# Weight sums in place, a fifth buffer of split weights, and interleaved halves of pairs in a decoder layer of float32 products

## The chip, the cores and the metric

The kernel runs on one core of a Trainium2 chip. The metric is the device time of one launch in microseconds (us), the median of several runs. The engines that matter here are TensorE (PE in the profile, its weight loads PEld), which does the matrix products; ScalarE (ACT) and VectorE (DVE), which prepare its operands; GpSimd (POOL), which issues accumulating transfers on a DMA queue of its own; and SyncE (SP), which issues the loads of all weights.

## The reference

One layer of a decoder, batch 1, 256 positions, model width 2048, in float32:

```
x = x + 0.5 * swiglu(rmsnorm(x, g1), wg1, wu1, wd1)     # swiglu(h) = (silu(h @ wg) * (h @ wu)) @ wd
h = rmsnorm(x, gm);  parts = split(h @ w_in)            # attention and mLSTM inputs
x = x + concat(diff_attention(parts), mlstm(parts)) @ w_out
x = x + 0.5 * swiglu(rmsnorm(x, g2), wg2, wu2, wd2)
return rmsnorm(x, g_final)
```

The hidden width of the two gated feed-forward blocks (FFN 1 and FFN 2) is 5632: 44 rows of 128, or 11 chunks of 512 columns. Each of their six weight matrices has 46 MB and is read once. The change is in the FFNs alone.

## The kernel before

**Products of split numbers.** Every float32 operand is split into a high part (a cast on ScalarE, L113) and a low part (the difference, on VectorE, L114), and each product is three TensorE instructions: high times high (L141), high times low (L142), low times high (L143). The weights are the moving operand, 512 columns wide (128x512, 256 KB of float32 for 128 rows). So each weight has to be loaded, cast and subtracted before TensorE can use it, and the split weights live in the pool wsp, whose buffers (four before) hold two 128x512 tiles, high and low, of "one split".

**Pairs: seven products in place of eight.** The 256 positions are two halves of 128. The class Paired takes two columns of weights wa and wb (gate and up for one chunk of the hidden width, or two chunks of the down matrix) and computes both for both halves. A pair is two rows k, k+1 of both columns, a 2x2 block: B11 = wa row k, B21 = wa row k+1, B12 = wb row k, B22 = wb row k+1. The activations are combined beforehand (A1, A2, B2 and S1 to S4). The weights of a pair are combined here:

- f, one split of two sums: T1 = B11+B12 for the accumulator p5 and T3 = B22+B12 for p7. Before, both are written by one VectorE instruction (L350) to a tile "sums" of the pool wrp (five buffers, which the single units below use too);
- e, one split of B11 for p1 and T2 = T1+B22 for p6 (T2 by VectorE, L352, in B12's place);
- bare, one split of B21 and T4 = T2+B21. T4 is made by an accumulating DMA on GpSimd's queue, 256 KB from one part of the raw tile to another (L361), which adds B21 to T2 in place, once e has read T2;
- upper, one split of the B22 of two pairs.

first() does f and e of each pair of a run, then combine() (L368 to L373) forms sums of the four accumulators: u1 is a copy of p1 (L368, L371 are ScalarE's copies), u2 = p6 + u1 (L369), p7 += u2 (L370), u3 is a copy of p7 (L371), and two subtractions into p6 and p5 (L372, L373). Then second() adds bare, upper and the single units of column wa (p1 and p7), after which these two accumulators are complete; the single units of column wb are left as a stream, third(), that goes on p5 and p6.

**Order.** Chain.run pulls a run's first() one step at a time and between the steps takes from the stream that the run before has left, so that each step of first() is followed by its share of single units. A generator's `yield` is where the stream's units come in. In each FFN there are 18 or 19 runs: 10 or 11 of gate and up (four pairs and four streamed units), and 8 of down, two (c = 0 and c = 2) for each of the four parts into which the hidden width is cut, with three pairs in parts 0 to 2 (and three units of each column) and one pair in part 3 (six chunk rows left as units). That makes 37 runs and 122 pairs.

The order of instructions on each engine is set by a scheduler from the order of the code and from priorities: loads, sums and splits stand under tc.high_priority(AHEAD), 400 places ahead of their place in the code, the combine under soon(), 440 places ahead. On the chip each engine then works through its list in order, and each instruction waits for its semaphores. SyncE's loads wait for a free tile of their pool: wr (four raw tiles of 1 MB, one for each pair) or wrp (tiles of 512 KB: single units, and the sums).

Of the kernel before, what the change touches and what calls it, by code (L numbers as in the profile page):

```python
# [17 lines left out]
P = 128  # L18
# [6 lines left out]
CW = 512  # L25
# [24 lines left out]
def tile_trunk_layer(ctx: ExitStack, tc: tile.TileContext, x, xt, par, bias_if, lamv, fnorm,  # L50
# [6 lines left out]
    wr = ctx.enter_context(tc.tile_pool(name="wr", bufs=4))  # L57
    wrp = ctx.enter_context(tc.tile_pool(name="wrp", bufs=5))
    wsp = ctx.enter_context(tc.tile_pool(name="wsp", bufs=4))
    small = ctx.enter_context(tc.tile_pool(name="small", bufs=2))  # L60
# [103 lines left out]

    def load_pair(dst, w, k):
        nc.sync.dma_start(dst, w[k // LK][:, k % LK:k % LK + 2, :])  # L166

    def load_unit(w, k):
        raw = wrp.tile([P, UK, CW], F32, tag="rawp", name=nm("rawp"))
        with tc.high_priority(offset=AHEAD):  # L170
            load_pair(raw, w, k)
        return raw
# [149 lines left out]
    class Paired:  # L322
# [4 lines left out]

        def __init__(self, xp, wa, wb, nk, ns, w0=0):
            self.xp, self.wa, self.wb, self.k0 = xp, wa, wb, w0 * LK
            self.ns, self.rest = ns, range(2 * ns, nk, UK)  # L330
            self.raws = []

        def prod(self, acc, j, xi, w, wi, first, last, on=False):
            xh, xl = self.xp[j]
            mm3(acc, xh[:, xi, :], xl[:, xi, :], w[0][:, wi, :], w[1][:, wi, :], first, last, on)

        def first(self):


            self.p1, self.p6, self.p7, self.p5 = (bank() for _ in range(4))  # L340
            for j in range(self.ns):
                raw = wr.tile([P, 4, CW], F32, tag="raw", name=nm("raw"))
                self.raws.append(raw)
                at, end = j == 0, j == self.ns - 1
                with tc.high_priority(offset=AHEAD):
                    for i, w in enumerate((self.wa, self.wb)):
                        load_pair(raw[:, 2 * i:2 * i + 2, :], w, self.k0 + 2 * j)
                    f = pair_tiles(wsp, "w", [P, 2, CW])
                    sums = wrp.tile([P, 2, CW], F32, tag="rawp", name=nm("sums"))
                    nc.vector.tensor_tensor(out=sums, in0=raw[:, 0:4:3, :],  # L350
                                            in1=raw[:, 2:3, :].to_broadcast([P, 2, CW]), op=ALU.add)
                    nc.vector.tensor_tensor(out=raw[:, 2, :], in0=sums[:, 0, :], in1=raw[:, 3, :], op=ALU.add)  # L352
                    e = pair_tiles(wsp, "w", [P, 2, CW])
                    split(sums, *f)
                    split(raw[:, 0:3:2, :], *e)
                self.prod(self.p5, j, S1, f, 0, at, end)
                self.prod(self.p7, j, S3, f, 1, at, end)
                self.prod(self.p1, j, A1, e, 0, at, end)
                self.prod(self.p6, j, S2, e, 1, at, end)
                with tc.high_priority(offset=AHEAD):  # L360
                    nc.gpsimd.dma_start(raw[:, 2, :], raw[:, 1, :], accum_op=ALU.add)  # L361
                yield
# [23 lines left out]
        def second(self):  # L386
# [3 lines left out]
            def bare(j):  # L390
                with tc.high_priority(offset=AHEAD):
                    t = pair_tiles(wsp, "w", [P, 2, CW])
                    split(self.raws[j][:, 1:3, :], *t)
                self.prod(n11, j, A2, t, 0, False, False, True)
                self.prod(n21, j, B2, t, 1, False, False, True)

            def upper(j0):
                with tc.high_priority(offset=AHEAD):
                    t = pair_tiles(wsp, "w", [P, 2, CW])
                    js = range(j0, min(j0 + 2, self.ns))  # L400
                    for i, j in enumerate(js):
                        split(self.raws[j][:, 3, :], t[0][:, i, :], t[1][:, i, :])
                for i, j in enumerate(js):
# [58 lines left out]
    def ffn(chain, xp, rstd, wg, wu, wd, finish, first=None):  # L462
# [21 lines left out]
        for part, (n, ns) in enumerate(zip(PARTS, NP_DOWN)):  # L484
# [19 lines left out]
            for c in (0, 2):  # L504
                p = Paired(hid, wd[c], wd[c + 1], n * 4, ns, done)
                if last:
# [517 lines left out]
```

## Time and profile before

The median of three runs is 1823.52 us (1822.75 to 1824.73). The page describes one profiled execution.

| | before |
|---|---|
| profiled execution, device time | 1824.08 us |
| its span in the trace | 1822.4 us |
| granted clock of TensorE, mean | 0.998 |
| TensorE busy | 1794.6 us (98%) in 8090 instructions |
| VectorE busy | 1488.8 us (82%) |
| ScalarE busy | 1121.7 us (62%) |
| GpSimd busy | 156.3 us (9%) |
| queue of the loads, share of 16 DMA engines | 55.5% |
| GpSimd's queue, share of 16 DMA engines | 14.2% |
| read from HBM | 349.56 MB |

How to read it: a row of the waits names the waiting engine, the tile and line that waits, then what it waited for, the time in us, the number of waits and the longest one. A row of the order of time has the start (us from the span's start), the duration, the engine, the line, the operation, what it writes and reads with shapes, and in brackets how long the engine stood before it and for what. A row of the table by stretches has the stretch, its length, the busy time and number of instructions of PE, PEld, DVE, ACT and POOL, TensorE's granted clock, the busy share of the DMA engines, and GB/s.

### The profile page before, as it was taken

What the parts mean: (1) busy time and instruction counts of PE and PEld (TensorE: products, weight loads), DVE (VectorE), ACT (ScalarE), POOL (GpSimd) and SP (SyncE); (2) the same over time, 40 slices, a digit from 0 to 9 for tenths busy, and PEclk for the clock granted to TensorE, in tenths of its full rate; (3) what the DMA queues carried; (4) which work ended last, traced back from release to release, by engine and by line L of the source; (5) the groups of instructions that cost most, each with busy time, mean ns of one, the idle gap of its engine ahead of it and who ended that gap; (6) DMA issues with size and microseconds to landing.
All of it is one profiled execution on the core that took longest, in us unless ns stands there. A gap on an engine that the chain in (4) does not pass through costs nothing.

```text
span 1822.4 us, 22684 instructions
## 1 busy us (share of the span) xinstructions
PE 1794.6 (98%) x8090; PEld 1468.2 (81%) x8090; DVE 1488.8 (82%) x1775; ACT 1121.7 (62%) x1443; POOL 156.3 (9%) x199
## 2 busy tenths in 40 slices
PE   8999999999999999999999999999999999999998
PEld 6788788878887888978888888788787888887886
DVE  6889889988998887674465578899889988998886
ACT  6666666666666666554455456666666666666664
POOL 0001100111002100000000000101110021002100
PEclk9999999999999999999999999999999999999999
DMA  8667877797688874553544565677877798678864
GB/s 333 215 204 235 222 234 232 246 250 220 210 252 247 259 237 146 200 185 121 185 159 164 185 213 179 199 228 241 234 230 225 256 247 243 208 230 256 253 190 155
DMA packets 114449, 397.72 MB, mean 218 GB/s; under 512 B 12960, under 2 KB 12960, under 8 KB 107424
## 3 DMA queue, kind: packets, MB, share of 16 engines
q1 hardware_dynamic: 88560, 349.28, 55.5%
q0 software_dynamic: 24480, 44.58, 14.2%
q10 hardware_dynamic: 1296, 2.42, 0.4%
q8 instruction: 63, 1.03, 0.2%
q14 instruction: 50, 0.41, 0.1%
HBM read 349.56 MB, written 2.10 MB: 193 GB/s over the span
## 4 chain that ended last, share of the span: by engine, by line
PE 76%; DMA 9%; DVE 8%; issue 4%; ACT 2%; SPq 1%; POOL 0%; POOLq 0%; DVEq 0%; ACTq 0%
PE acc L142 24%; PE acc L143 24%; PE acc L141 24%; DMA raw<-in_wu_dram 6%; DVE wl L114 5%; ACT wh L113 2%; DVE sums L350 2%; DMA raw<-raw 1%; PE tr L296 1%; SPq L166 1%; DMA xres<-in_x_dram 1%; DVE raw L352 1%; DMA xraw<-in_xt_dram 1%; DMA raw<-in_wd_dram 0%; PE num L808 0%
## 5 line engine op out<-in xcount | busy, mean ns | idle before, releaser
L113 ACT CAST wh<-raw 128x1024 fp32r<-128x1024 f32 (+3 forms) x503 | 464.3, 931 | 377.2 <-PE acc L143 360.9
L114 DVE TENSOR_TENSOR wl<-raw,wh 128x1024 fp32r<-128x1024 f32 (+3 forms) x503 | 535.1, 1074 | 194.7 <-ACT wh L113 191.1
L142 PE MATMUL acc<-wl,xt 128*128 128x512 f32 (+3 forms) x1632 | 630.4, 386 | 4.2 <-DVE wl L114 4.0
L141 PE MATMUL acc<-wh,xt 128*128 128x512 f32 (+3 forms) x1632 | 630.7, 387 | 2.6 <-ACT xt L108 1.5
L143 PE MATMUL acc<-wh,xt 128*128 128x512 f32 (+3 forms) x1632 | 628.8, 386 | 1.2 <-DVE xt L109 1.2
L114 DVE TENSOR_TENSOR wl<-rawp,wh 128x1024 fp32r<-128x1024 f32 x284 | 346.7, 1222 | 43.8 <-ACT wh L113 37.1
L113 ACT CAST wh<-rawp 128x1024 fp32r<-128x1024 f32 x284 | 298.8, 1053 | 117.1 <-PE acc L143 96.4
L141 PE MATMUL acc<-wh,xs 128*128 128x512 f32 x902 | 355.7, 397 | 8.4 <-ACT wh L113 4.0
L142 PEld LDWEIGHTS acc<-wl,xt 128*128 128x128 f32 x1632 | 306.5, 188 | 67.9 <-DVE wl L114 8.8
L141 PEld LDWEIGHTS acc<-wh,xt 128*128 128x128 f32 x1632 | 306.0, 188 | 65.5 <-ACT wh L113 2.8
L143 PEld LDWEIGHTS acc<-wh,xt 128*128 128x128 f32 x1632 | 306.3, 188 | 62.1 <-DVE xt L109 2.5
L142 PE MATMUL acc<-wl,xs 128*128 128x512 f32 x902 | 352.7, 391 | 1.3 <-DVE wl L114 1.1
L143 PE MATMUL acc<-wh,xs 128*128 128x512 f32 x902 | 350.9, 390 | 0.1
L113 ACT CAST wh<-sums 128x1024 fp32r<-128x1024 f32 x122 | 128.4, 1053 | 144.4 <-PE acc L143 139.2
L141 PEld LDWEIGHTS acc<-wh,xs 128*128 128x128 f32 x902 | 169.1, 188 | 57.2 <-ACT u L371 9.3
L142 PEld LDWEIGHTS acc<-wl,xs 128*128 128x128 f32 x902 | 169.4, 188 | 38.9 <-DVE wl L114 6.4
L143 PEld LDWEIGHTS acc<-wh,xs 128*128 128x128 f32 x902 | 169.3, 188 | 36.0 <-DVE xs L109 1.0
L361 POOL DMA_DIRECT2D raw<-raw x122 | 104.0, 853 | 1030.9 <-DVE wl L114 973.7
L350 DVE TENSOR_TENSOR sums<-raw 128x1024 f32<-128x1024 f32 x122 | 149.2, 1223 | 39.4 <-DMA raw<-in_wu_dram 29.2
L114 DVE TENSOR_TENSOR wl<-sums,wh 128x1024 fp32r<-128x1024 f32 x122 | 149.0, 1222 | 14.7 <-ACT wh L113 14.7
L352 DVE TENSOR_TENSOR raw<-sums,raw 128x512 f32<-128x512 f32 x122 | 83.8, 687 | 0.5
L282 POOL DMA_DIRECT2D xres<-part x48 | 43.6, 1060 | 238.2 <-ACT part L281 238.2
(194 smaller groups left out, 756.0 us busy)
## 6 DMA issues: line engine op xcount, KB each, us to landing
rawp<-in_wd_dram SPq DMA_DIRECT2D x96, 512.0 KB, 5.7
rawp<-in_wu_dram SPq DMA_DIRECT2D x94, 512.0 KB, 7.6
raw<-in_wg_dram SPq DMA_DIRECT2D x89, 512.0 KB, 6.7
rawp<-in_wg_dram SPq DMA_DIRECT2D x86, 512.0 KB, 5.7
raw<-in_wu_dram SPq DMA_DIRECT2D x82, 512.0 KB, 7.5
raw<-in_wd_dram SPq DMA_DIRECT2D x80, 512.0 KB, 6.3
raw<-in_win_dram SPq DMA_DIRECT2D x40, 1024.0 KB, 4.8
raw<-raw POOLq DMA_DIRECT2D x122, 256.0 KB, 6.3
```

The costliest lines, as they stand in the source:

```text
L113: nc.scalar.copy(hi, src)
L114: nc.vector.tensor_tensor(out=lo, in0=src, in1=hi.bitcast(F32), op=ALU.subtract)
L141: nc.tensor.matmul(acc, lh, rh, start=first, stop=False, skip_group_check=on)
L142: nc.tensor.matmul(acc, lh, rl, start=False, stop=False, skip_group_check=on)
L143: nc.tensor.matmul(acc, ll, rh, start=False, stop=last, skip_group_check=on)
L166: nc.sync.dma_start(dst, w[k // LK][:, k % LK:k % LK + 2, :])
L282: nc.gpsimd.dma_start(xres[:, hb, c * CW:(c + 1) * CW], t, accum_op=ALU.add)
L296: nc.tensor.transpose(tr[:, i, hb * P:(hb + 1) * P], hs[hb][:, k * P:(k + 1) * P], ident)
L350: nc.vector.tensor_tensor(out=sums, in0=raw[:, 0:4:3, :], in1=raw[:, 2:3, :].to_broadcast([P, 2, CW]), op=ALU.add)
L352: nc.vector.tensor_tensor(out=raw[:, 2, :], in0=sums[:, 0, :], in1=raw[:, 3, :], op=ALU.add)
L361: nc.gpsimd.dma_start(raw[:, 2, :], raw[:, 1, :], accum_op=ALU.add)
```

## The change

Sums in place. The raw tile of a pair has four places of 256 KB. B11 is loaded to place 3, B12 and B22 to places 1 and 2 by one load of 512 KB. One VectorE instruction writes T3 and T1 to places 0 and 1 (L351 of the changed kernel): the tile "sums" is gone. Once f has split them, T2 = T1 + B22 is made in place 1 (L357; a branch that would let a DMA do it is in the code, but its argument by_dma is False in every run). B21 is loaded late, as a load of its own of 256 KB, to place 0, after f's split has read T3 from there; then GpSimd's accumulating DMA adds it to T2 in place 1 (L371), once e's split has read T2.

Buffers. wsp has five buffers instead of four; wrp has three instead of five.

Order. e of pair j-1 comes after f of pair j, and the places of the `yield`, at which streamed units come in, move. Of three pairs the order is now f0, units, f1, e0, f2, e1, units, e2, units; of four f0, units, f1, e0, units, f2, e1, f3, e2, units, e3, units; of one f0, units, e0. Before it was f0, e0, units, f1, e1, units and so on. bare and upper read other places of the raw tile. The lines of the combine are L387 to L392 now (u2 L388, p7 L389, u3 L390).

```
-    wrp = ctx.enter_context(tc.tile_pool(name="wrp", bufs=5))
-    wsp = ctx.enter_context(tc.tile_pool(name="wsp", bufs=4))
+    wrp = ctx.enter_context(tc.tile_pool(name="wrp", bufs=3))
+    wsp = ctx.enter_context(tc.tile_pool(name="wsp", bufs=5))
...
-    def load_pair(dst, w, k):
-        nc.sync.dma_start(dst, w[k // LK][:, k % LK:k % LK + 2, :])
+    def load_rows(dst, w, k, n):
+        nc.sync.dma_start(dst, w[k // LK][:, k % LK:k % LK + n, :])
...
         def first(self):
             self.p1, self.p6, self.p7, self.p5 = (bank() for _ in range(4))
-            for j in range(self.ns):
+            def f(j):
                 raw = wr.tile([P, 4, CW], F32, tag="raw", name=nm("raw"))
                 self.raws.append(raw)
                 at, end = j == 0, j == self.ns - 1
                 with tc.high_priority(offset=AHEAD):
-                    for i, w in enumerate((self.wa, self.wb)):
-                        load_pair(raw[:, 2 * i:2 * i + 2, :], w, self.k0 + 2 * j)
-                    f = pair_tiles(wsp, "w", [P, 2, CW])
-                    sums = wrp.tile([P, 2, CW], F32, tag="rawp", name=nm("sums"))
-                    nc.vector.tensor_tensor(out=sums, in0=raw[:, 0:4:3, :],
-                                            in1=raw[:, 2:3, :].to_broadcast([P, 2, CW]), op=ALU.add)
-                    nc.vector.tensor_tensor(out=raw[:, 2, :], in0=sums[:, 0, :], in1=raw[:, 3, :], op=ALU.add)
-                    e = pair_tiles(wsp, "w", [P, 2, CW])
-                    split(sums, *f)
-                    split(raw[:, 0:3:2, :], *e)
-                self.prod(self.p5, j, S1, f, 0, at, end)
-                self.prod(self.p7, j, S3, f, 1, at, end)
-                self.prod(self.p1, j, A1, e, 0, at, end)
-                self.prod(self.p6, j, S2, e, 1, at, end)
+                    load_rows(raw[:, 3:4, :], self.wa, self.k0 + 2 * j, 1)
+                    load_rows(raw[:, 1:3, :], self.wb, self.k0 + 2 * j, 2)
+                    t = pair_tiles(wsp, "w", [P, 2, CW])
+                    nc.vector.tensor_tensor(out=raw[:, 0:2, :], in0=raw[:, 2:4, :],
+                                            in1=raw[:, 1:2, :].to_broadcast([P, 2, CW]), op=ALU.add)
+                    split(raw[:, 0:2, :], *t)
+                    if self.by_dma and j < self.ns - 1:
+                        nc.gpsimd.dma_start(raw[:, 1, :], raw[:, 2, :], accum_op=ALU.add)
+                    else:
+                        nc.vector.tensor_tensor(out=raw[:, 1, :], in0=raw[:, 1, :], in1=raw[:, 2, :], op=ALU.add)
+                self.prod(self.p5, j, S1, t, 1, at, end)
+                self.prod(self.p7, j, S3, t, 0, at, end)
+
+            def e(j):
+                raw = self.raws[j]
+                at, end = j == 0, j == self.ns - 1
                 with tc.high_priority(offset=AHEAD):
-                    nc.gpsimd.dma_start(raw[:, 2, :], raw[:, 1, :], accum_op=ALU.add)
+                    t = pair_tiles(wsp, "w", [P, 2, CW])
+                    split(raw[:, 1:4:2, :], *t)
+                self.prod(self.p1, j, A1, t, 1, at, end)
+                self.prod(self.p6, j, S2, t, 0, at, end)
+                with tc.high_priority(offset=AHEAD):
+                    load_rows(raw[:, 0:1, :], self.wa, self.k0 + 2 * j + 1, 1)
+                    nc.gpsimd.dma_start(raw[:, 1, :], raw[:, 0, :], accum_op=ALU.add)
+
+            for j in range(self.ns):
+                f(j)
+                if j:
+                    e(j - 1)
+                if j != self.ns - 2:
+                    yield
+            e(self.ns - 1)
+            if self.ns > 1:
                 yield
...
-                    split(self.raws[j][:, 1:3, :], *t)
+                    split(self.raws[j][:, 0:2, :], *t)
...
-                        split(self.raws[j][:, 3, :], t[0][:, i, :], t[1][:, i, :])
+                        split(self.raws[j][:, 2, :], t[0][:, i, :], t[1][:, i, :])
```

How the order moves. VectorE in FFN 1, the second down run (c = 2) of part 0, three pairs. Before, from e of pair 1 (its raw tile is raw_302) to p7 of the combine; raw_293 and raw_311 are the raw tiles of pairs 0 and 2, rawp a single unit, L350 and L352 the sums of the next run:

```order
L114 TENSOR_TENSOR wl_307_1538<-raw_302_1529,wh_306_1537 128x1024
L114 TENSOR_TENSOR wl_310_1559<-rawp_308_1556,wh_309_1558 128x1024
L114 TENSOR_TENSOR wl_313_1578<-sums_314_1579,wh_312_1577 128x1024
L350 TENSOR_TENSOR sums_353_1752<-raw_350_1747 128x1024
L114 TENSOR_TENSOR wl_316_1583<-raw_311_1574,wh_315_1582 128x1024
L114 TENSOR_TENSOR wl_319_1604<-rawp_317_1601,wh_318_1603 128x1024
L352 TENSOR_TENSOR raw_350_1747<-sums_353_1752,raw_350_1747 128x512
L114 TENSOR_TENSOR wl_326_1635<-raw_293_1484,wh_325_1634 128x1024
L114 TENSOR_TENSOR wl_329_1647<-rawp_327_1644,wh_328_1646 128x1024
L369 TENSOR_TENSOR u2_321_1620<-acc_290_1481,u1_320_1619 128x512
L114 TENSOR_TENSOR wl_331_1663<-raw_302_1529,wh_330_1662 128x1024
L370 TENSOR_TENSOR acc_291_1482<-acc_291_1482,u2_321_1620 128x512
```

After, the same stretch; the raw tiles of pairs 0, 1 and 2 are raw_284, raw_290 and raw_295:

```order
L114 TENSOR_TENSOR wl_299_1560<-raw_290_1517,wh_298_1559 128x1024
L114 TENSOR_TENSOR wl_302_1574<-rawp_300_1571,wh_301_1573 128x1024
L114 TENSOR_TENSOR wl_304_1590<-raw_295_1544,wh_303_1589 128x1024
L114 TENSOR_TENSOR wl_307_1604<-rawp_305_1601,wh_306_1603 128x1024
L114 TENSOR_TENSOR wl_314_1635<-raw_284_1484,wh_313_1634 128x1024
L114 TENSOR_TENSOR wl_317_1647<-rawp_315_1644,wh_316_1646 128x1024
L114 TENSOR_TENSOR wl_319_1663<-raw_290_1517,wh_318_1662 128x1024
L388 TENSOR_TENSOR u2_309_1620<-acc_281_1481,u1_308_1619 128x512
L114 TENSOR_TENSOR wl_321_1673<-raw_284_1484,wh_320_1672 128x512
L389 TENSOR_TENSOR acc_282_1482<-acc_282_1482,u2_309_1620 128x512
```

The first row of each list is the low part of e of pair 1. The second split from the same raw tile is bare of pair 1 (wl_331 before, wl_319 after). Nine rows stand between the two before, five after: f of pair 2 and the next run's sums are no longer among them. u2, the first VectorE step of the combine, stands one row ahead of that bare before, and one row behind it after.

VectorE in FFN 1, the first down run of part 3 (one pair). Before, from e (raw_1178 is the raw tile of the only pair) to bare:

```order
L114 TENSOR_TENSOR wl_1183_5649<-raw_1178_5640,wh_1182_5648 128x1024
L114 TENSOR_TENSOR wl_1186_5670<-rawp_1184_5667,wh_1185_5669 128x1024
L114 TENSOR_TENSOR wl_1189_5688<-rawp_1187_5685,wh_1188_5687 128x1024
L114 TENSOR_TENSOR wl_1192_5706<-rawp_1190_5703,wh_1191_5705 128x1024
L369 TENSOR_TENSOR u2_1197_5740<-acc_1175_5637,u1_1196_5739 128x512
L114 TENSOR_TENSOR wl_1195_5724<-rawp_1193_5721,wh_1194_5723 128x1024
L370 TENSOR_TENSOR acc_1176_5638<-acc_1176_5638,u2_1197_5740 128x512
L350 TENSOR_TENSOR sums_1225_5852<-raw_1222_5847 128x1024
L372 TENSOR_TENSOR acc_1175_5637<-acc_1177_5639,u3_1198_5741 128x512
L373 TENSOR_TENSOR acc_1177_5639<-acc_1177_5639,u2_1197_5740 128x512
L114 TENSOR_TENSOR wl_1200_5751<-raw_1178_5640,wh_1199_5750 128x1024
```

After; raw_1122 is the pair's raw tile, L313 the gated products of the run before:

```order
L114 TENSOR_TENSOR wl_1136_5712<-rawp_1134_5709,wh_1135_5711 128x1024
L114 TENSOR_TENSOR wl_1138_5728<-raw_1122_5640,wh_1137_5727 128x1024
L114 TENSOR_TENSOR wl_1143_5751<-raw_1122_5640,wh_1142_5750 128x1024
L114 TENSOR_TENSOR wl_1145_5761<-raw_1122_5640,wh_1144_5760 128x512
L114 TENSOR_TENSOR wl_1148_5770<-rawp_1146_5767,wh_1147_5769 128x1024
L313 SCALAR_TENSOR_TENSOR sg_1116_5632<-acc_1049_5279,rstd_53_356,sg_1116_5632 128x512
L313 SCALAR_TENSOR_TENSOR sg_1117_5634<-acc_1047_5277,rstd_53_356,sg_1117_5634 128x512
```

Before, four splits of units and the steps of the combine stand between e and bare of the only pair. Now bare follows e directly, and u2 comes after the gated products.

7 lines of the change are left out of this document (4 added, 3 removed).

## The prediction

> **What bounds the kernel now.** I read the page first, then the waits of TensorE, then the order of time around the places where a pair's halves end.
>
> ```profile
> span 1822.4 us, 22684 instructions
> PE 1794.6 (98%) x8090; PEld 1468.2 (81%) x8090; DVE 1488.8 (82%) x1775; ACT 1121.7 (62%) x1443; POOL 156.3 (9%) x199
> PEld acc L142 <- DVE wl L114: 15.1, 25, 1.2
> PEld acc L141 <- ACT wh L113: 10.9, 15, 1.6
> PEld acc L141 <- ACT u L371: 9.3, 25, 1.3
> ACT wh L113 <- PE acc L143: 596.5, 594, 4.3
> 361.00:379.00 18.00, 18.00 (x80) 14.69 (x79) 16.24 (x18) 11.93 (x16) 3.34 (x4) 1.00 0.72 183
> 497.50:532.00 34.50, 34.50 (x158) 28.53 (x157) 33.55 (x39) 22.61 (x27) 2.55 (x3) 1.00 0.84 262
> 569.00:603.60 34.60, 34.02 (x149) 27.26 (x148) 29.74 (x32) 22.40 (x27) 6.86 (x8) 1.00 0.92 259
> ```
>
> TensorE is the bound: it is busy 98% of the span at the full granted clock, and in a stretch without a gap 80 matmuls take 18.0 us, one each 0.226 us. The change leaves their number as it is, so it can only move the gaps. Weights that come late (rows two and three of the waits) hold TensorE's weight loads for 15.1 + 10.9 = 26.0 us in the whole span: no gain can be larger. ScalarE stands 596.5 us in casts that wait for a buffer of split weights to come free, so the four buffers, not ScalarE, set how far the splits run ahead. The last two rows are stages: in 497.5 to 532 us VectorE works 33.55 of 34.50 us, and in 569 to 603.6 us the DMA engines are 92% busy. So three resources stand just behind TensorE.
>
> **What stays the same.** VectorE's work is the same in kind and number.
>
> ```profile
> L350 DVE TENSOR_TENSOR sums<-raw 128x1024 f32<-128x1024 f32 x122 | 149.2, 1223 | 39.4 <-DMA raw<-in_wu_dram 29.2 <-DMA raw<-in_wd_dram 5.5 <-DVE wl L114 2.7
> L352 DVE TENSOR_TENSOR raw<-sums,raw 128x512 f32<-128x512 f32 x122 | 83.8, 687 | 0.5
> L369 DVE TENSOR_TENSOR u<-acc,u 128x512 f32<-128x512 f32 x37 | 25.3, 684 | 0.0
> L371 ACT COPY u<-acc 128x512 f32<-128x512 f32 x37 | 21.4, 579 | 0.6 <-DVE acc L370 0.4
> L313 DVE SCALAR_TENSOR_TENSOR sg<-acc,rstd,sg 128x512 f32<-128x512 f32 x44 | 31.9, 744 | 0.0
> ```
>
> The two sums cost 1.22 us a pair at L350, and T2 0.69 us at L352. The changed kernel does both with as many elements, in place, and the trace has no in-place row to say otherwise; I take the same 1.22 and 0.69. The bytes loaded are the same too. What changes is when things may start.
>
> **Term A: six runs of three pairs with three streamed units** (the second down run of parts 0 to 2, in both FFNs). T4 of each pair is made by an accumulating DMA, which can start once the split e has read T2. So far e follows f directly. Now e of pair 1 comes after f of pair 2, while the combine (u2, p7, u3), on which the second half's products on p7 wait, has moved behind the split of T4 of pair 1 on VectorE, and u1 behind its cast on ScalarE. The run around 360 us, before:
>
> ```profile
> 358.13 1.22 DVE L114 TENSOR_TENSOR wl<-sums,wh 128x1024 fp32r<-128x1024 f32 x1
> 359.26 1.22 DVE L114 TENSOR_TENSOR wl<-raw,wh 128x1024 fp32r<-128x1024 f32 x1
> 361.53 0.69 DVE L352 TENSOR_TENSOR raw<-sums,raw 128x512 f32<-128x512 f32 x1
> 362.13 1.22 DVE L114 TENSOR_TENSOR wl<-sums,wh 128x1024 fp32r<-128x1024 f32 x1
> 363.27 1.22 DVE L114 TENSOR_TENSOR wl<-raw,wh 128x1024 fp32r<-128x1024 f32 x1
> 375.00 0.68 DVE L369 TENSOR_TENSOR u<-acc,u 128x512 f32<-128x512 f32 x1
> 360.56 0.39 PE L142 MATMUL acc<-wl,xs 128*128 128x512 f32 x1
> 378.53 0.50 PE L141 MATMUL acc<-wh,xs 128*128 128x512 f32 x1
> 360.78 1.02 POOL L361 DMA_DIRECT2D raw<-raw  x1
> 364.79 0.84 POOL L361 DMA_DIRECT2D raw<-raw  x1 [1.56 <-DVE wl L114]
> DMA to landing us min/median/max: 7.8/7.8/7.8
> DMA to landing us min/median/max: 9.0/9.0/9.0
> 1651.40 9.57 DMA raw<-raw
> 374.20 1.05 ACT L113 CAST wh<-raw 128x1024 fp32r<-128x1024 f32 x1
> ```
>
> VectorE rows follow each other 1.13 us apart at 1024 elements (358.13, 359.26) and 0.60 at 512 (361.53, 362.13). f of pair 0 ends at 359.35, 1.2 us before its first use at 360.56. e of pair 1 ends at 364.49, its DMA is issued 0.3 us later, and the two landings (GpSimd at 360.78, then at 364.79) take 7.8 and 9.0 us; in the same run at 1651 us the second takes 9.57. So T4 of pair 1 lands at 373.8, and u2 at 375.0 and the products on p7 at 378.53 are not held by it.
>
> Afterwards, between f of pair 0 and e of pair 1 VectorE has six rows of 1024 and three of 512: 6 x 1.13 + 3 x 0.60 = 8.6 us. TensorE comes to e of pair 1 after 36 products, 8.2 us. So e of pair 1 leads its use by 1.2 - 0.4 = 0.8 us. From its end: issue 0.3, landing 8.6 (between the 7.8 of the first and the 9.0 to 9.6 of the second), cast 1.05, split 1.22, u2 0.60, a 512 split 0.60, p7 0.69, u3 0.58, sum 13.6 us. TensorE's cover is the products from e of pair 1 (its second) to the first on p7: 5 + 12 + 6 + 12 + 8 = 43, 9.7 us. The gap is 13.6 - 9.7 - 0.8 = 3.1 us, six times 18.6 us. Bounds: with the buffers as the only limit e could lead by 4.2 us (its buffer comes free 30 products, 6.8 us, earlier, less cast, split and latency), which with a landing of 7.8 leaves nothing; with no lead and 9.6 it is 4.9 us. So 0 to 29 us.
>
> The Trainium skill's page "DMA: Bandwidth & Descriptors", section "Anatomy of one DMA — SWDGE (gpsimd) path", fits a DMA of this queue as 2.0 us plus its bytes over 436 GB/s; for 256 KB that is an estimate of 2.6 us, by which the gap and with it term A would be nothing. The rows above, 7.8 to 9.57 us, speak against it here.
>
> **Term B: the one-pair runs** (part 3). Before, f and e came first and the four streamed units covered the DMA. Now e comes after the units, and right behind it on VectorE stands the split of T4, then an upper split, a unit's split and the two gated products, for whose transposes TensorE waits next.
>
> ```profile
> 660.57 1.22 DVE L114 TENSOR_TENSOR wl<-raw,wh 128x1024 fp32r<-128x1024 f32 x1
> 662.08 0.84 POOL L361 DMA_DIRECT2D raw<-raw  x1 [25.07 <-DVE wl L114]
> DMA to landing us min/median/max: 7.3/7.3/7.3
> 669.43 1.05 ACT L113 CAST wh<-raw 128x1024 fp32r<-128x1024 f32 x1 [2.25 <-DVE acc L370]
> DMA to landing us min/median/max: 6.5/6.5/6.5
> ```
>
> Here the issue at 662.08 lands 7.3 us later, at 669.4, and the cast starts with it; in FFN 2 (issue at 1758.52) it takes 6.5. Chain after e's split: 0.3 + 6.9 + cast 1.05 + split 1.22 + 0.60 + 1.13 + 2 x 0.70 = 12.6 us. Cover: e's six products 1.4 us and its lead; e's buffer is f's, free 48 products, 10.9 us, before, less cast, split and latency 8.4 us. Gap 2.8 us, twice 5.6 us; a row of another one-pair run has 4.6 us, which gives 0.5 each, and a lead of 6.5 us gives 4.7: 1 to 9 us. The second one-pair runs must also load B21 after f before T4; their cover (74 products and three transposes from p7's first to the split's use, 18 us) about equals load, accumulate and splits; I take 0.5 each, 1 us, bounds 0 and 4.
>
> **Term C: what the fifth buffer and the later B21 save.**
>
> ```profile
> DVE sums L350 <- DMA raw<-in_wu_dram: 29.2, 22, 2.6
> 388.81 1.23 DVE L350 TENSOR_TENSOR sums<-raw 128x1024 f32<-128x1024 f32 x1 [1.61 <-DMA raw<-in_wu_dram]
> 288.91 1.05 ACT L113 CAST wh<-sums 128x1024 fp32r<-128x1024 f32 x1 [0.30 <-PE acc L143]
> 290.01 0.50 PE L141 MATMUL acc<-wh,xs 128*128 128x512 f32 x1 [0.62 <-ACT wh L113]
> SPq L166 <- DVE wl L114: 1098.4, 289, 11.8
> DMA to landing us min/median/max: 3.3/6.3/9.9
> ```
>
> Sums wait 29.2 us for loads, as at 388.81, after four 512 KB loads; 768 KB a pair is needed first now, not 1 MB. Of some five such stages I expect 1 us each. At 288.91 a cast waits for a buffer and TensorE for the cast; five such gaps of 0.8 us are what a fifth buffer takes away. Together 9 us, bounds 0 and 26.0. Two tiles fewer for single units (five shared with the sums, now three) cost nothing as I take it: SyncE already waits 1098.4 us for a tile to come free, and three units of TensorE work, 3 x 2.7 = 8.2 us, cover a load and its splits; if that cover goes, one late load costs the 1 to 2 us that late sums cost here.
>
> **Sum.** 18.6 + 5.6 + 1.0 - 9.0 = +16.2 us. The profiled execution took 1824.08 us (span 1822.4 and 1.7 around it), 0.56 above the median of 1823.52. So 1840.3 against it, 1840 for the median.
>
> **The rivals.**
> T4 lands in time (faster). In the planned order the combine sits behind the split as if T4 were there. If accumulates land within some 5.5 us (over all 122 of L361 the last row gives 3.3 us at least, 6.3 in the middle and 9.9 at most), term A is gone, B falls to 1 and the gains remain, perhaps 11: 1824 - 10 = 1814. This is also where the skill's fit of 2.6 us points. Against it: the landings of 9.0 and 9.57 us, with residual sums ahead in GpSimd's queue, which stay there. 0.24.
> Gains and losses cancel: VectorE, let ahead by the fifth buffer, leads e of pair 1 by some 3 us. A 1 us a run, 6, B 3, C 9: 1824. 0.13.
> The fifth buffer gives nothing, because VectorE, 97% busy in the stage at 497.5 us, cannot fill it: C is 0, 1849. 0.13.
> The 21 gate and up runs are held too. There also u2 stands behind the split of T4 of pair 1, and 56 products, 12.7 us, cover a chain of 0.3 + 7.4 + 1.05 + 1.22 + 0.60 + 0.74 + 0.69 + 0.58 = 12.6 us: nothing, as long as landings stay at 7.4 us or below. If the late B21 loads, in the stage with 92% busy DMA engines above all, add 0.7 us, 21 runs lose some 15 us: 1855. 0.08.
>
> **How the numbers follow.** The forecast holds 0.42 and has 1832 to 1848 as its own range (A between 2 and 4 us a run). With the two slower rivals, slower by over 0.2% (3.6 us, about what a measurement of this kernel can tell) has 0.63; no change has 0.13; faster has 0.24. The range reaches to the faster rival's middle and to the gate rival: 1814 to 1855.
>
> **What would show it.** In the changed profile, u2 (then L388) would wait for the split of T4, and the weight loads behind u3 (then L390) would wait for some 3 us in six runs, with GpSimd's accumulates still landing after 8 us or more; before the transposes of the one-pair runs TensorE would stand some 3 us. Waits for wl and wh elsewhere should fall from 26.0 by some 9 us. I am wrong if TensorE has no gap over 1 us at the six combines, or if accumulates land in 5 us, or if the gaps sit in the gate and up runs.

## The result and the profile after

The changed kernel takes 1841.4 us (median of four runs, 1838.2 to 1844.5), the kernel before 1823.7 us (1822.8 to 1824.7). The ratio is 1.0097, with a 95% interval of 1.0079 to 1.0115: slower by about 18 us. The forecast was 1840. The number came out; the next rows show that most of its reasons did not. The profile is of the fastest of the four, 1838.2 us.

The page of the changed kernel, its span and first row:

```profile
span 1836.5 us, 23011 instructions
PE 1793.8 (98%) x8090; PEld 1469.3 (80%) x8090; DVE 1482.0 (81%) x1775; ACT 1114.4 (61%) x1443; POOL 156.3 (9%) x199
```

TensorE is busy for 1793.8 us, 0.8 less than before, and the span is 14.1 us longer: the loss lies in gaps. What TensorE's matmuls waited for, first before, then after (waiting engine and tile, releaser, us in total, times, longest):

```profile
PE acc L142 <- DVE wl L114: 5.1, 12, 0.8
PE acc L141 <- ACT wh L113: 4.9, 9, 0.7
PE acc L141 <- ACT u L371: 1.3, 2, 0.9
```

```profile
PE acc L141 <- ACT xs L113: 10.3, 7, 2.0
PE acc L142 <- DVE wl L114: 9.1, 14, 1.4
PE acc L143 <- DVE xt L114: 3.2, 5, 1.1
PE acc L141 <- ACT u L390: 2.7, 4, 1.1
PE tr L296 <- DVE sg L313: 2.2, 4, 1.2
PE acc L141 <- ACT wh L113: 1.9, 2, 1.3
```

The largest row is 10.3 us for xs, the split sums of activations (L271 to L276); the kernel before has 0.3 us for them, on a weight load, and nothing on a matmul. Six of the seven waits, 8.5 us together, are for sums of hidden activations; the first, 1.80 us at 52 us, is for sums of the block's input. With it comes xt, the split of unpaired hidden rows, 3.2 us. All rows of the matmuls' waits add up to 18.2 us before and 33.3 us after, so xs and xt are 13.5 of the 15.1 us more. The matmuls' waits for weights (wl and wh) did not fall: 10.0 us before, 11.0 after. Waits for u3 (L390), where the forecast put its largest term, grew by 1.4 us only; they are taken apart below.

One of the seven xs waits, at 334 us (first down run of part 1). VectorE and ScalarE in the kernel before, in order of time: the split of hg, the first and last of a pair's sums, and their cast.

```profile
312.68 0.69 DVE L114 TENSOR_TENSOR xs<-hg,xs 128x512 fp32r<-128x512 f32 x1
313.28 0.42 DVE L273 TENSOR_TENSOR xsum<-hg 128x256 f32<-128x256 f32 x1
321.53 0.29 DVE L275 TENSOR_TENSOR xsum<-hg,xsum 128x128 f32<-128x128 f32 x1
321.85 0.62 ACT L113 CAST xs<-xsum 128x512 fp32r<-128x512 f32 x1
```

The same pair in the changed kernel, with the matmul that needs it:

```profile
317.88 0.68 DVE L114 TENSOR_TENSOR xs<-hg,xs 128x512 fp32r<-128x512 f32 x1
329.08 0.42 DVE L273 TENSOR_TENSOR xsum<-hg 128x256 f32<-128x256 f32 x1
333.09 0.28 DVE L275 TENSOR_TENSOR xsum<-hg,xsum 128x128 f32<-128x128 f32 x1
333.40 0.62 ACT L113 CAST xs<-xsum 128x512 fp32r<-128x512 f32 x1 [1.84 <-DVE xsum L275]
334.07 0.50 PE L141 MATMUL acc<-wh,xs 128*128 128x512 f32 x1 [1.61 <-ACT xs L113]
```

The source of the sums, hg, is there by 317.88 in the changed kernel, since its own split runs then; but the first sum runs at 329.08 and the last at 333.09, with weight sums and weight splits ahead of them in VectorE's list. Before, the first sum came 0.60 us after that split started. So the operand is 11.6 us later (333.40 against 321.85), and TensorE stands 1.61 us for it.

### The profile page after: what moved, and what is told of

Its sections match the earlier page's. It is cut to its first block, busy times and chain, and to the rows that moved or that the text cites. A ratio compares the mean times of both kernels' runs of the same rounds, so it can differ in the third digit from the quotient of the medians.

```text
span 1836.5 us, 23011 instructions
## 1 busy us (share of the span) xinstructions
PE 1793.8 (98%) x8090; PEld 1469.3 (80%) x8090; DVE 1482.0 (81%) x1775; ACT 1114.4 (61%) x1443; POOL 156.3 (9%) x199
## 5 line engine op out<-in xcount | busy, mean ns | idle before, releaser
L113 ACT CAST wh<-raw 128x1024 fp32r<-128x1024 f32 (+2 forms) x625 | 589.9, 955 | 415.0 <-PE acc L143 279.1
L114 DVE TENSOR_TENSOR wl<-raw,wh 128x1024 fp32r<-128x1024 f32 (+2 forms) x625 | 679.4, 1100 | 195.7 <-ACT wh L113 190.8
L141 PE MATMUL acc<-wh,xs 128*128 128x512 f32 x902 | 356.9, 396 | 16.5 <-ACT xs L113 10.3
L141 PEld LDWEIGHTS acc<-wh,xs 128*128 128x128 f32 x902 | 169.2, 188 | 61.9 <-ACT xs L113 13.6
L351 DVE TENSOR_TENSOR raw<-raw 128x1024 f32<-128x1024 f32 x122 | 149.2, 1223 | 81.9 <-DMA raw<-in_wu_dram 63.2
L371 POOL DMA_DIRECT2D raw<-raw x122 | 103.8, 851 | 978.5 <-DVE wl L114 572.2
L357 DVE TENSOR_TENSOR raw<-raw 128x512 f32<-128x512 f32 x122 | 83.6, 686 | 1.1
L113 ACT CAST xs<-xsum 128x512 fp32r<-128x512 f32 x28 | 17.3, 620 | 32.1 <-DVE xsum L275 32.1
L313 DVE SCALAR_TENSOR_TENSOR sg<-acc,rstd,sg 128x512 f32<-128x512 f32 x44 | 32.5, 743 | 0.0
```

Of the source, the lines that this page charges most:

```text
L113: nc.scalar.copy(hi, src)
L114: nc.vector.tensor_tensor(out=lo, in0=src, in1=hi.bitcast(F32), op=ALU.subtract)
L141: nc.tensor.matmul(acc, lh, rh, start=first, stop=False, skip_group_check=on)
L313: nc.vector.scalar_tensor_tensor(s, src, r, s, op0=ALU.mult, op1=ALU.mult)
L351: nc.vector.tensor_tensor(out=raw[:, 0:2, :], in0=raw[:, 2:4, :], in1=raw[:, 1:2, :].to_broadcast([P, 2, CW]), op=ALU.add)
L357: nc.vector.tensor_tensor(out=raw[:, 1, :], in0=raw[:, 1, :], in1=raw[:, 2, :], op=ALU.add)
```

## The experiments

Four theories stood against each other. Theory O: the interleaving itself, with its stretches of pairs without units. Theory B: the fifth buffer, which lets weight splits pass the activation work in the lists. Theory L: the late load of B21. Theory D, formed after the first runs: T2, written over T1, has to wait until f's low part is made. "Before" in each ratio is the kernel before, run beside it. It took 1823.7 us beside the changed kernel and 1825.1 to 1826.6 us in the later sets of runs, so a difference between times of two sets is good to some 3 us.

**The order of before, five buffers** (label e1). f and e of a pair together, a unit after each pair:

```
             for j in range(self.ns):
                 f(j)
-                if j:
-                    e(j - 1)
-                if j != self.ns - 2:
-                    yield
-            e(self.ns - 1)
-            if self.ns > 1:
-                yield
+                e(j)
+                yield
```

> The changed kernel with f and e of each pair together and a streamed unit after each pair, as before; sums in place, late B21 and five buffers of split weights stay. Theory O (the interleaving is the cause: f2 e1 f3 e2 without a unit give VectorE 2 x 4.0 us of sums and splits for 5.4 us of products, so that it falls behind and the activation sums xs and weight splits come late): the 10.3 us of TensorE waiting for xs (L113) fall below 2 us, the time to 1822 to 1829 us. Theory B (the fifth buffer lets weight splits go ahead of the activation sums in VectorE's list): xs waits stay at 8 us or more, 1836 us or above. Theory L (the late B21, its own small loads): weights' waits stay, 1834 us or above.

Measured 1914.5 us, ratio 1.0478 (1.0441 to 1.0514): 73 us slower than the changed kernel. Only the open ends of B and L ("or above") reach so far; none had the size. No wait for the casts of xs is left, as theory O had it and B had not, but the time went the other way. What TensorE's matmuls waited for most among work on activations:

```profile
PE acc L141 <- ACT sg L309: 24.9, 8, 4.5
PE acc L143 <- DVE xt L114: 15.9, 6, 3.2
```

Both are work without the weights' priority. ScalarE's waits, after (first row) and in this run (second):

```profile
ACT wh L113 <- DVE raw L357: 86.2, 60, 3.8
```

```profile
ACT wh L113 <- DVE raw L357: 237.0, 75, 10.2
```

The cast of e waits for T2 (L357). T2 overwrites the place of T1, and f's low part, a VectorE instruction that itself waits for ScalarE's cast, still reads T1. So the chain sum, cast of f, low part of f, T2, cast of e runs through both engines one step at a time. Before, T2 went to another place than the sums, and casts waited for it 0.9 us in all. Theory O falls as the cause of the loss: the interleaving covers this chain, as it puts f of the next pair between f and e.

**Four buffers, interleaved** (e2): `bufs=5` of wsp set to 4.

> The changed kernel with four buffers of split weights, as before; the interleaving stays. Theory O: VectorE has less lead with which to meet the stretches of pairs without units, 1845 to 1855 us, TensorE's waits for wl of raw tiles above 15 us. Theory B: the activation sums come in time again, xs waits below 3 us, 1826 to 1833 us. Theory L: no change, 1838 to 1844 us.

Measured 1874.6 us, ratio 1.0271 (1.0247 to 1.0294), 33 us above the changed kernel and slower than any theory said. TensorE's waits:

```profile
PE acc L142 <- DVE wl L114: 32.0, 22, 3.8
PE acc L141 <- ACT xs L113: 0.3, 1, 0.3
```

Both halves matter. With four buffers the activation sums come in time (0.3 us against 10.3), as theory B had it; and the weights come late (32.0 us against 9.1). The fifth buffer trades one for the other. Theory B's time, 1826 to 1833 us, was missed.

**The order of before, four buffers** (e3): both edits.

> The changed kernel with the order of before and four buffers: sums in place and late B21 alone (wrp stays at three). Theories O and B: 1822 to 1830 us, and as far above the run with the old order and five buffers as the fifth buffer is worth (0 to 5 us). Theory L: 1836 us or above, with the waits of L351 for loads of wu still near 63 us.

Measured 1913.9 us, ratio 1.0481 (1.0460 to 1.0503). All theories but L had expected about 1826, and the waits of L351 for loads of wu (61.5 us) are where L had them; but L is not shown by that, as the next pair of runs tells. ScalarE waits 247.9 us for T2 here. Beside e1 the trade of the fifth buffer shows again: with four buffers the matmuls wait 6.9 us for sg and not at all for xt (40.8 us for both in e1), but 45.4 us for weights (23.5 in e1), and the time is the same.

**T2 in a place of its own** (e5 on the order of before, e6 interleaved, both with four buffers). The raw tile gets a fifth place; T2 goes there, and so do T4 and the splits that read them:

```
-                raw = wr.tile([P, 4, CW], F32, tag="raw", name=nm("raw"))
+                raw = wr.tile([P, 5, CW], F32, tag="raw", name=nm("raw"))
...
-                        nc.vector.tensor_tensor(out=raw[:, 1, :], in0=raw[:, 1, :], in1=raw[:, 2, :], op=ALU.add)
+                        nc.vector.tensor_tensor(out=raw[:, 4, :], in0=raw[:, 1, :], in1=raw[:, 2, :], op=ALU.add)
...
-                    nc.gpsimd.dma_start(raw[:, 1, :], raw[:, 0, :], accum_op=ALU.add)
+                    nc.gpsimd.dma_start(raw[:, 4, :], raw[:, 0, :], accum_op=ALU.add)
```

> The run with the old order and four buffers, with one thing taken away: T2 is written to a fifth place of the raw tile, so that it and the cast of e no longer wait for f's low part, which reads T1 in the place that T2 overwrites. T1 and T3 in place, the late B21 and wrp of three stay. Theory D (that wait, 247.9 us of ScalarE standing for L357, makes the old order slow): the time falls from 1913.9 to 1822 to 1832 us and the wait for L357 below 20 us. Theory L (the late B21 and its accumulate): 1895 us or above, the weights' waits on TensorE still over 40 us.

> The interleaved order with four buffers (1874.6 us) and T2 in a place of its own. Theory D with the interleaving as a mere cover for the wait: the interleaving now costs or brings little beside the old order with T2 in its own place, both within 10 us of each other. Theory O (the stretches without units cost by themselves): 1860 us or above, TensorE still waiting over 25 us for wl of raw tiles.

Measured 1861.1 us (ratio 1.0206, 1.0175 to 1.0236) and 1845.8 us (1.0106, 1.0080 to 1.0133). Freeing T2 brings 52.8 us in the order of before (from 1913.9) and 28.8 us interleaved (from 1874.6). Theory D is shown, though not as all of the loss: e5 stays 36 us above the kernel before, where 1822 to 1832 had been expected. The interleaving is worth 39 us while T2 waits and 15 us when it does not, where theory D had the two runs within 10 us; theory O's 1860 us for e6 did not come. L351's waits for loads of wu, L's sign in e3, fall from 61.5 to 32.1 us in e5, where B21 is loaded as late as in e3. ScalarE's and TensorE's waits in e5:

```profile
ACT wh L113 <- DVE raw L357: 1.2, 4, 0.3
ACT wh L113 <- DMA raw<-raw: 25.5, 8, 4.9
PE acc L141 <- ACT u L385: 15.1, 6, 3.4
```

The last row is the wait that the prediction's term A named, in another kernel: six waits for the copy u3, in the combines of the six second down runs of three pairs, 15.1 us together. Casts wait for T4 there (second row), although e stands right behind f: f of the next pair is not what makes T4 late in that run.

**B21 early** (e9). Four buffers, interleaved, B21 loaded with the rest of the pair into the fifth place, T2 over T1 as in the change; compare e2:

```
                     load_rows(raw[:, 1:3, :], self.wb, self.k0 + 2 * j, 2)
+                    load_rows(raw[:, 4:5, :], self.wa, self.k0 + 2 * j + 1, 1)
...
-                    load_rows(raw[:, 0:1, :], self.wa, self.k0 + 2 * j + 1, 1)
-                    nc.gpsimd.dma_start(raw[:, 1, :], raw[:, 0, :], accum_op=ALU.add)
+                    nc.gpsimd.dma_start(raw[:, 1, :], raw[:, 4, :], accum_op=ALU.add)
```

> The interleaved order with four buffers (1874.6 us), with B21 loaded together with the other three into a fifth place of the raw tile instead of late into the place of T3; T2 stays in T1's place. Theory L (the late load delays T4): 1855 us or below, the casts' waits for T4 (16.4 us) gone. Theory D (T2's wait alone): 1868 to 1880 us, as T2 still waits for f.

Measured 1880.3 us (1.0298, 1.0272 to 1.0324) against 1874.6. In the interleaved order with four buffers loading B21 early brings nothing; theory L falls there. ScalarE's wait for T4 is 15.1 us, as it was with the late load (16.4).

**Activation sums ahead** (e4). The changed kernel, and the copy, sums and splits of paired hidden rows under the weights' priority:

```
             if j < ns:
                 g = wk("hg")
-                nc.scalar.copy(g, tr.rearrange("p a b -> p (a b)"))
-                sum_pair(hid, j, g.rearrange("p (a b) -> p a b", b=P))
+                with tc.high_priority(offset=AHEAD):
+                    nc.scalar.copy(g, tr.rearrange("p a b -> p (a b)"))
+                    sum_pair(hid, j, g.rearrange("p (a b) -> p a b", b=P))
```

> The changed kernel with the copy, sums and splits of the hidden activations (sum_pair in hid_transposes) under the same priority as the weight splits. Theories O and B: the waits for xs and for the low parts of xt, 10.3 + 3.2 us, fall below 3 us and the time to 1827 to 1833 us; if VectorE is simply too slow in those stretches, the gap only moves to the weight splits and the time stays at 1836 us or above. Theory L: 1838 to 1844 us.

Measured 1822.0 us, ratio to before 0.9977 (0.9961 to 0.9993): 19.4 us below the changed kernel (22 us by the two ratios), more than the 13.5 us of xs and xt that it was aimed at. TensorE's waits, and the sum and cast of the pair shown above:

```profile
PE acc L143 <- DVE xt L114: 6.0, 5, 1.9
PE acc L142 <- DVE wl L114: 4.1, 6, 1.1
PE tr L296 <- DVE sg L314: 3.5, 4, 1.6
PE acc L141 <- ACT xs L113: 0.6, 1, 0.6
312.15 0.28 DVE L275 TENSOR_TENSOR xsum<-hg,xsum 128x128 f32<-128x128 f32 x1
312.47 0.62 ACT L113 CAST xs<-xsum 128x512 fp32r<-128x512 f32 x1 [0.51 <-DVE xsum L275]
```

The sums are done 21 us earlier, the waits for xs are nearly gone (0.6 us, for the block's input), and the waits for weights did not grow but fell from 9.1 to 4.1 us. So VectorE had room for both; it was the order of its list. The waits for xt grew from 3.2 to 6.0, so that side of the expectation was missed.

**All hidden work ahead** (e7): in addition the splits of unpaired rows, and the gated products 300 places ahead of the weights' priority in place of 40.

```
-                split(tr, *plain_pair(hid, j))
+                pp = plain_pair(hid, j)
+                with tc.high_priority(offset=AHEAD):
+                    split(tr, *pp)
...
-                with soon():
+                with soon(300):
                     hs = [gated(au[hb], r[:, hb:hb + 1], sg[hb]) for hb in range(NT)]
```

> The changed kernel with all work on hidden activations ahead: the sums and splits as in the run with xs ahead (1822.0 us), the splits of unpaired hidden rows under the same priority too, and the gated products 300 places further ahead. If list positions on VectorE are what is left of the loss: the waits for xt's low part (6.0 us) and of the transposes for sg (3.5 us) fall below 2 us together, 1812 to 1818 us. If VectorE is full there, the waits move to the weight splits: 1820 us or above.

Measured 1822.9 us (0.9978, 0.9964 to 0.9992): no better than e4. The waits for xt went, but those for sg grew to 4.5 us, for wl to 5.8 us and for u to 4.4 us in two rows.

**The kernel before, with activation sums ahead** (e8), the edit of e4 alone:

> The kernel before with the hidden activations' sums under the weight splits' priority, nothing else. If late activation sums are a loss only of the changed kernel's list: no change, 1821 to 1827 us. If they were a cost in the kernel before too, 1812 to 1818 us.

Measured 1826.5 us (1.0006, 0.9992 to 1.0020): no change. The late sums are a fault of the changed kernel's list alone.

**The kernel before, with five buffers** (e10): `bufs` of wsp 4 to 5 and of wrp 5 to 3.

> The kernel before with five buffers of split weights and three tiles in wrp (units and sums together), nothing else. By the prediction's term C, which gave the fifth buffer the most of 9 us: 1816 to 1822 us. If in the kernel before the splits are not held by the number of buffers, or three tiles in wrp hold the sums: 1825 us or above.

Measured 1829.5 us (1.0013, 0.9993 to 1.0033): no change that can be told. TensorE's weight loads and matmuls waited for:

```profile
PEld acc L142 <- DVE wl L114: 6.9, 19, 1.0
PE acc L141 <- ACT part L281: 5.3, 6, 2.1
PE acc L141 <- ACT u L371: 3.1, 7, 1.0
PE acc L141 <- ACT sg L309: 3.1, 4, 1.4
```

The weight loads' waits for weights (wl, and wh with 3.2 us) fell from 26.0 to 10.1 us, more than term C expected. At the matmuls they fell from 10.0 to 2.2 us, and as much came back as waits for work on activations that TensorE gets from ScalarE: part, u and sg have 11.5 us (u and sg had 1.3 and 0.8 us before, part no row). The edit also takes wrp from five tiles to three; the two are not separated.

**Units spread evenly** (e11), in the changed kernel:

```
             for j in range(self.ns):
                 f(j)
                 if j:
                     e(j - 1)
-                if j != self.ns - 2:
                     yield
             e(self.ns - 1)
-            if self.ns > 1:
-                yield
+            yield
```

> The changed kernel with the streamed units spread evenly: f0 f1 e0 unit f2 e1 unit f3 e2 unit e3 unit, and f0 f1 e0 unit f2 e1 unit e2 unit. Theory O (stretches without a unit leave VectorE behind): the weight waits in the gate and up runs (wl of raw tiles, 9.1 us of TensorE) fall below 5 us, 1832 to 1838 us. If the spacing is not the cause: 1839 us or above.

Measured 1839.4 us (1.0075, 1.0052 to 1.0098), no different from the changed kernel's 1841.4 within the intervals; its waits for wl are 9.9 us, not below 5. So the spacing is not the cause of those waits, and theory O falls in this form too. The waits for xs did fall, from 10.3 to 6.1 us. The edit also puts e of a one-pair run right behind f; the waits of transposes for sg are gone here too, as in the next run.

**One-pair runs in the order of before** (e12), on top of e4:

```
-                if j != self.ns - 2:
+                if j != self.ns - 2 and self.ns > 1:
                     yield
             e(self.ns - 1)
-            if self.ns > 1:
-                yield
+            yield
```

> The run with xs ahead (1822.0 us), and the runs of one pair with e straight after f, ahead of the units, as before. By the prediction's term B (2.8 us in each first run of one pair, 5.6 to 6.6 us in all): 1814 to 1818 us, the transposes' wait for the gated products (3.5 us) gone. Theory D: e of the only pair then has f's chain in front of it with no cover, 2 to 3 us in each of four runs: 1822 to 1834 us.

Measured 1818.0 us, ratio 0.9950 (0.9931 to 0.9970), 4.0 us below e4, and no row for sg is left among TensorE's waits. The intervals of the two ratios still overlap slightly (0.9961 to 0.9970), so the 4 us rest on the rows as much as on the times. This version is faster than both kernels of the case: 8.4 us below the kernel before in the same set of runs.

## Why the prediction was right in its number and wrong in its reasons

**What bounds the kernel.** Right: TensorE's work is unchanged, and the loss is in gaps. The bound of 26.0 us for what earlier weights can save holds. That only gaps can move is not quite right; see the last section.

**The sums in place cost nothing more by themselves.** Right in duration, wrong in what they make wait. L351 and L357 take 1223 and 686 ns on average, the 1.22 and 0.69 us taken over from L350 and L352. The step that failed is "What changes is when things may start": it was followed for loads and for T4, not for T2, which now waits for f's low part. e5 and e6 put 53 and 29 us on that wait with four buffers; in the changed kernel, where casts wait 86.2 us for T2, its price was not measured.

**Term A (18.6 us): the mechanism is real, the size was not.** The same combine that the prediction worked out, the second down run of part 1, in the changed kernel:

```profile
364.92 1.22 DVE L114 TENSOR_TENSOR wl<-raw,wh 128x1024 fp32r<-128x1024 f32 x1
369.58 0.39 PE L141 MATMUL acc<-wh,xs 128*128 128x512 f32 x1
367.52 0.84 POOL L371 DMA_DIRECT2D raw<-raw  x1 [2.96 <-DMA raw<-in_wd_dram]
DMA to landing us min/median/max: 6.1/6.1/6.1
373.86 1.05 ACT L113 CAST wh<-raw 128x1024 fp32r<-128x1024 f32 x1 [1.66 <-PE acc L143]
374.95 1.22 DVE L114 TENSOR_TENSOR wl<-raw,wh 128x1024 fp32r<-128x1024 f32 x1 [1.49 <-ACT wh L113]
376.09 0.68 DVE L388 TENSOR_TENSOR u<-acc,u 128x512 f32<-128x512 f32 x1
378.90 0.57 ACT L390 COPY u<-acc 128x512 f32<-128x512 f32 x1
379.55 0.47 PE L141 MATMUL acc<-wh,xs 128*128 128x512 f32 x1
187.52 0.50 PE L141 MATMUL acc<-wh,xs 128*128 128x512 f32 x1 [0.55 <-ACT u L390]
1289.97 0.50 PE L141 MATMUL acc<-wh,xs 128*128 128x512 f32 x1 [0.31 <-ACT u L390]
```

The rows are e of pair 1 (VectorE), its first matmul, its accumulate with its landing, the cast and low part of bare of pair 1, u2, u3 and the matmul that needs u3; the last two rows are the only waits for u3 at the six combines. VectorE does stand 1.49 us before the split of T4 with u2 behind it, as forecast, though the cast it waits for is put down to a buffer of split weights, T4 having landed at 373.6. The issue comes 1.4 us after the split, not 0.3, since it waits for the late B21; the landing takes 6.1 us, not 8.6; u3 starts 0.9 us after p7, as a cast stands ahead of it on ScalarE. Together these nearly cancel: from the end of e's split (366.14) to the end of u3 (379.47) it is 13.3 us, where the forecast had 13.6, and the cover from 369.58 to 379.55 is 10.0 us, where it had 9.7.

The step that failed is "So e of pair 1 leads its use by 1.2 - 0.4 = 0.8 us". The lead is 369.58 - 366.14 = 3.4 us, nearer to the bound of 4.2 that the buffers set, and 13.3 - 10.0 - 3.4 leaves no gap; at the six combines, read in the same way, it is 2.9 to 3.6 us. The 0.8 was worked out from the kernel before, with its four buffers. In e6, the same order with four buffers and T2 free, it about holds. The low part of e of pair 1, its first matmul and the wait for u3, in the second down run of part 0:

```profile
182.18 1.21 DVE L114 TENSOR_TENSOR wl<-raw,wh 128x1024 fp32r<-128x1024 f32 x1
183.95 0.39 PE L141 MATMUL acc<-wh,xs 128*128 128x512 f32 x1
195.20 0.50 PE L141 MATMUL acc<-wh,xs 128*128 128x512 f32 x1 [1.11 <-ACT u L390]
```

The lead is 183.95 - 183.39 = 0.6 us there and 0.5 to 1.6 us at the six combines of e6, and three of them wait for u3, 5.1 us together. In e2, which differs from the changed kernel in the buffers alone, it is -0.2 to 1.0 us. So it is the fifth buffer that lets e come early enough.

So at the six combines of the changed kernel the waits are 0.55 + 0.31 = 0.9 us, not 18.6, and by its own test the forecast is wrong here. The page's other two waits for u3, 1.11 and 0.72 us, stand in the second one-pair runs. In e5, where no pair separates f from e, the gap is there, six times, 15.1 us.

**Term B (5.6 + 1.0 us): about right in its sum.** The waits of transposes for sg are 2.2 us in the changed kernel, against 5.6, and in the second one-pair runs 2.6 us for u1 and u3, against 1.0: 4.8 us together. In e4 the waits for sg are 3.5 us; undoing the order in e12 brought 4.0 us, within the intervals of the two ratios.

**Term C (-9.0 us): half there at the weight loads, not at the matmuls, and it came with a price that was not looked for.** The weight loads' waits went from 15.1 + 10.9 to:

```profile
PEld acc L142 <- DVE wl L114: 17.6, 21, 1.7
PEld acc L141 <- ACT wh L113: 3.1, 3, 1.8
PEld acc L141 <- ACT xs L113: 13.6, 8, 2.5
PEld acc L143 <- DVE xt L114: 6.2, 7, 1.5
```

20.7 us in place of 26.0, 5.3 saved of the 9 forecast; against them stand 19.8 us of xs and xt, where before has 0.3. A weight load's wait is not yet a gap of the matmuls (at 334.07 us 2.03 us of the one left 1.61 us of the other): the matmuls' own waits for weights went from 10.0 to 11.0 us, and nothing was saved there. The step that failed: the fifth buffer was counted as room for weights only. It also moves weight work ahead of everything with a lower priority in the lists of VectorE and ScalarE, and e2 (xs wait 0.3 us with four buffers), e4 (the list mended: -19.4 us) and e10 (the same trade in the kernel before) show it. Which work comes late depends on the order as well: in e1, also with five buffers, it is sg and xt, and not xs.

**The rivals.** "T4 lands in time" was right in its mechanism, with accumulates at 4.4 us in the middle, a second of the forecast's own signs of being wrong; at the combine shown, with a landing of 6.1 us, it was e's lead that brought T4 in time. It was wrong in its time, since the activation sums took the place. The Trainium skill's page "DMA: Bandwidth & Descriptors", section "Anatomy of one DMA — SWDGE (gpsimd) path", pointed to that rival; the estimate of 2.6 us for 256 KB by its fit lies below the shortest landing here.

```profile
DMA to landing us min/median/max: 3.3/4.4/9.2
```

"Gains and losses cancel" had the lead right, 3 us against the 3.4 measured, and it too left out the activation sums. "The fifth buffer gives nothing" was right for the kernel before in its time, and wrong in its ground: VectorE could use the buffer. "Gate and up runs are held by T4" is not seen: the 9.1 us of waits for wl do stand in those runs, but ahead of their combines, and not behind u3.

**So the sum was right by accident.** 18.6 us of which 0.9 were there stand against 13.5 us of waits for xs and xt that had not been thought of, and of the saving of 9 us the matmuls show nothing.

**What stays open.** Why the order of before with T2 free (e5) still takes 36 us more than the kernel before: 15.1 us are the u3 waits, but the three tiles of wrp, T1 and T3 in place, and the late B21 in that order were not separated. What T2's place costs in the changed kernel itself, with five buffers, was not run, nor was wrp of five. Why the accumulates land faster than before (4.4 us against 6.3) was not tried; in the runs with f and e together the middle is 5.1 to 5.6 us, and interleaved with four buffers 4.0 to 4.6. And 9.1 us of waits for wl in the changed kernel have no single cause shown, except that they fell to 4.1 with the activation sums moved.

## What to carry to other kernels

Writing a result over an operand saves a tile and adds a wait: look up who still reads the operand, and on which engine that reader waits in turn. A buffer more for prioritized work is also a push of everything without priority to the back of the same engine's list; look there for the next wait, and give what TensorE needs next the same priority. A lead worked out from the kernel before does not hold when the change adds a buffer. A forecast that hits its number has still to be checked place by place: here its largest term, 18.6 us, came out at 0.9.

## What the runs showed that was not expected

A gap on TensorE can be followed by a slower clock, and then costs more than its length. In the changed kernel, around its longest wait on xs, TensorE's wait in order of time and then the table by stretches (length, busy time and number of instructions of PE, PEld, DVE, ACT and POOL, granted clock, DMA share, GB/s):

```profile
1436.62 0.50 PE L141 MATMUL acc<-wh,xs 128*128 128x512 f32 x1 [2.05 <-ACT xs L113]
```

```profile
1438.10:1441.50 3.40, 3.40 (x9) 2.63 (x8) 2.30 (x3) 1.99 (x2) 0.09 (x1) 0.50 0.94 252
```

Some 1.5 us after the wait of 2.05 us ends, the granted clock is 0.50 for 3.4 us, and 1.00 again from 1441.5: 9 instructions where at 0.226 us each 15 would fit, a further 1.4 us lost. In the run with the order of before and five buffers, where waits last up to 5.0 us, the mean clock falls to 0.982. An estimate from that, at most: 1.8% of its span of 1913.7 us, 34 us, against 5.5 us at the changed kernel's 0.997, so that up to some 29 of the 77 us between their spans are clock and not waiting. It counts the low clock also where TensorE has nothing to do, as in the last 5.8 us of the changed kernel (clock 0.50, no matmul). Not every gap of that length is followed by it. Counted from one matmul's start to the next, the gap above is 2.44 us; gaps of 2.19 and 2.12 us in the same kernel (at 50 and 1242 us) are not, nor is one of 3.6 us in the run with the order of before (at 1308 us). And in the kernel before the clock is 0.50 for 3.4 us at 821.8 us, in the part between the FFNs, with no such gap near it. So what makes the clock fall is not settled here. The changed kernel's four times go with the clock roughly: 1838.2 and 1841.3 us at 0.997, 1844.5 at 0.994, 1841.5 at 0.995. The Trainium skill's page "TensorE: Matmul & The Clock Gate", section "Part 1: The HAM clock gate", has the half clock and its window of about 3.4 us, and the rows agree with both; it has the clock fall after at least one idle window of that length, and here a wait of 2.05 us was followed by it.
